# Query and key features of a decoder layer: ten groups from weights stationary to tokens stationary, two at a time, with two of eight pairs of k-tiles by seven products

## The chip, the cores and the metric

The kernel runs on one core of one Trainium2 chip. The metric is the time of one execution on the device, in microseconds (us); the time before is the median of three runs, 1559.32 us (1559.26 to 1560.52). The core has a matrix engine (PE, with PEld loading its stationary operand), a vector engine (DVE), an activation engine (ACT), GpSimd (POOL) and a sync engine (SP) that issues the DMAs here. Matrix products land in PSUM, which the kernel uses as eight banks of 128 x 512 fp32.

## The reference, cut to what matters

One decoder layer, 256 tokens of width 2048, all in fp32:

```
proj = x @ w_in                      # q, k, v, o, gates of the mLSTM; q, k, v of the attention
y_m  = mlstm_mixer(q_m, k_m, v_m, o_m, i_m, f_m, conv, ...)   # conv and silu on q_m, k_m first
y_a  = dilated_attention(q_a, k_a, v_a, rel_bias)
x = layer_norm(ALPHA * x + concat(y_m, y_a) @ w_out)
q, k, v = x @ wq, mem @ wk, mem @ wv     # cross-attention into 256 memory tokens, 4 heads
x = layer_norm(ALPHA * x + softmax(q k^T) v @ wo)
x = layer_norm(ALPHA * x + (silu(x @ w1) * (x @ w3)) @ w2)   # hidden width 5632
```

The change touches six of the eight groups of 512 columns of `w_in` that make queries and keys (groups 2 and 3: attention heads 4 to 7; 4 and 5: query and key of mLSTM heads 0 and 1; 6 and 7: of mLSTM heads 2 and 3), all four groups of `wk`, and the order of one loop over `w2`.

## The kernel before, in words

**Three products for one.** A fp32 product is made of three products in a rounded format. `split` (L109) writes a tile as a high part (ACT) and the rest (DVE subtract); a product is high x high + high x low + low x high. The left operands (tokens) are held split, in an `Operand` (L120): part j holds k-tiles 2j and 2j+1. Weights are loaded as blocks `b` of two k-tiles (1 MB) and split on the fly into `wh` and `wl`, five buffers of each (`SPLIT`, L36), three raw buffers (`RAW`).

**Two layouts.** `gemm_tokens` (L260) keeps tokens stationary and streams 512 columns of weights: the result has tokens on the partitions. `gemm_features` (L382) keeps a 128 x 128 block of weights stationary and streams the tokens: for each k-tile and each of four blocks one matmul of 512 columns (high weights by both parts of the 256 tokens, L392) and one of 256 (low weights by the high tokens, L393). Its result has the features on the partitions, which is what scores, convolution and cross-attention keys want. `features` (L400) adds the two halves. Before, all query and key projections go this way, one group of 512 features at a time.

**Seven products for eight.** `gemm_seven` (L323) makes a 256 x 1024 result as 2 x 2 blocks. For a block `b` in its `plan` that is a plain number it makes the eight block products (24 matmuls of 512 columns); for a block in parentheses, "(b,)", it uses a Winograd-like scheme with seven (21 matmuls): sums of weight blocks are made on DVE (`sums`, L299), sums of token blocks lie ready (`mix`, L136; `mix_again`, L148, makes them from a split operand). It needs all eight PSUM banks: five of the pool `pg` (P2, P3, Q4, E, P1) and all three of the pool `ps` (P5, P7, Q6). After the last seven-step of the plan the function `early` moves P1, P5, P7, Q6 out (`into_rows`, L684, or `into_z`, L665); the other four banks are added at the end. The loop over the feed-forward weights (L988) uses it on two groups at a time, with `plan = [0, 1, (2,), 3, 4, (5,), 6, 7]`, and `hidden` (L946) then makes eight transposes of 128 x 128 on PE (L959). `w2_first` (L976) uses it on the first half of `w2`, twice (w2a0, w2a1).

**Who else wants the three banks of `ps`.** `attention` (L485) takes for each head a bank for the scores (`sc`, L491) and one for their transposes (`pt`, L509), and for each two heads one for the outputs (`po`, L487). `gates` (L523) takes pgate, pc and four times bc. `mlstm` (L598) takes four per head (ms, mh, md, mpt). `turned` (L421) takes one for four transposes.

**What sets the order.** The program is written as one stream; a planner turns it into one fixed order per engine, by its own estimate of when each operand and buffer is ready; among operations that are ready, the earlier in the program goes first. Around the change the stream is: group 0, group 1, values of attention (v0), attention of heads 0 to 3 (L782), groups 2 and 3 (L784), `gates` (L785), attention of heads 4 to 7 (L787), groups 4 and 5 (L801), v1, v2, mLSTM heads 0 and 1 (L818), groups 6 and 7 (L820), mLSTM heads 2 and 3 (L821), keys of the memory 0 and 1 (L834), the output projection (wo0, wo1), keys 2 and 3, the first norm, and so on. Each mLSTM group's convolution (`conv_silu`, L578) runs on DVE as soon as its group is there. SBUF slots of 128 x 1024 are handed out when the program is written, first freed first used.

Of the kernel before, what the change touches and what calls it, by code (L numbers as in the profile page):

```python
# [14 lines left out]
ALU = mybir.AluOpType  # L15
# [7 lines left out]
KT = D // P  # L23
# [27 lines left out]
def decoder_layer(ctx: ExitStack, tc: tile.TileContext, A):  # L51
    nc = tc.nc
    V, SC, G, T = nc.vector, nc.scalar, nc.gpsimd, nc.tensor
# [66 lines left out]
    class Operand:  # L120
# [11 lines left out]
        def put(self, j, src):  # L132

            split(*self.views(j), src.rearrange("p (s t) -> p s t", s=2))
# [65 lines left out]
    def fetch_pair(src, name):  # L200


        def get(b):
            w = wp.tile([P, 2, W], F32, tag="w", name=f"{name}w{b}", bufs=RAW)
            for c in range(2):
                nc.sync.dma_start(
                    out=w[:, :, c * 512 : (c + 1) * 512],
                    in_=src[c][b // 2][:, b % 2].rearrange("p (s c) -> p s c", s=2),
                )
            return w  # L210

        return get
# [169 lines left out]
    def gemm_features(op, src, name, load=None, last=False):  # L382

        banks = [bank(f"{name}b{f}") for f in range(4)]
        for n, wh, wl in weights(src, KT // 2, name, load):
            order = [(f, s) for f in range(4) for s in range(2)]
            if n == 0:
                order.sort(key=lambda x: x[1])
            for f, s in order:
                kt, cs = 2 * n + s, slice(s * 512 + f * P, s * 512 + (f + 1) * P)  # L390
                end = kt == KT - 1
                T.matmul(banks[f], wh[:, cs], op.both(kt), start=kt == 0, stop=end, skip_group_check=True)  # L392
                T.matmul(  # L393
                    banks[f][:, :S], wl[:, cs], op.get(kt, 0), start=False, stop=end, skip_group_check=True
                )
            if last:
                op.free(n)
        return banks

    def features(banks, name):  # L400

        out = []
        for j in range(2):
            t, r = slot(f"{name}t{j}"), slot(f"{name}r{j}")
            for s in range(2):
                cs = slice(s * S, (s + 1) * S)
                SC.copy(t[:, cs], banks[2 * j + s][:, S:])
                V.tensor_tensor(out=r[:, cs], in0=banks[2 * j + s][:, :S], in1=t[:, cs], op=ALU.add)
            free(t)
            out.append(r)  # L410
        return out
# [9 lines left out]
    def turned(rows, j, name):  # L421

        pt = sbank(name)
        for s in range(2):
            for m in range(2):
                at = (2 * j + s) * P
                T.transpose(pt[:, s * S + m * P : s * S + (m + 1) * P], rows[m][:, at : at + P], ident)
        return pt
# [8 lines left out]
        out=tri, in_=tri, pattern=[[1, P]], compare_op=ALU.is_ge, fill=NEG, base=0, channel_multiplier=-1  # L437
# [10 lines left out]
    xT = Operand("xT")  # L448
# [129 lines left out]
    def conv_silu(raw, ft, name):  # L578

        y, t = slot(f"cy{name}"), slot(f"ct{name}")  # L580
        for s in range(2):
            c, a = cw[:, ft + s], s * S
            CONV.tensor_scalar(
                out=y[:, a : a + S], in0=raw[:, a : a + S], scalar1=c[:, 3:4], scalar2=c[:, 4:5],
                op0=ALU.mult, op1=ALU.add,
            )
            for k in range(1, 4):
                CONV.scalar_tensor_tensor(
                    out=y[:, a + k : a + S], in0=raw[:, a : a + S - k], scalar=c[:, 3 - k : 4 - k],
                    in1=y[:, a + k : a + S], op0=ALU.mult, op1=ALU.add,  # L590
                )
# [92 lines left out]
    def into_rows(rows, name):  # L684


        def early(of):
            u = slot(f"{name}u")
            for m in range(2):
                rows.append([slot(f"{name}{m}{c}") for c in range(2)])  # L690
            (r11, r12), (r21, r22) = rows
            SC.copy(r11, of["P1"])
            V.tensor_tensor(out=u, in0=r11, in1=of["Q6"], op=ALU.subtract)
            V.tensor_tensor(out=r21, in0=u, in1=of["P7"], op=ALU.add)
            V.tensor_tensor(out=r12, in0=of["P5"], in1=u, op=ALU.subtract)
            V.tensor_tensor(out=r22, in0=r12, in1=of["P7"], op=ALU.subtract)
            free(u)

        return early

    class Norm:


# [47 lines left out]
        return op  # L751


    def in_features(i, load=None, last=False):
        return features(gemm_features(xT, A["w_qk"][i], f"i{i}", load, last), f"i{i}")

    def in_rows(i):
        return gemm_tokens(xT, A["w_v"][i], KT, f"v{i}")
# [22 lines left out]
    va = rows_of(in_rows(0), "va")  # L781
    for j in range(2):  # L782
        attention(2 * j, qk0[j], qk0[2 + j], [va[m][0] for m in range(2)], tb)
    qk1 = in_features(2) + in_features(3)  # L784
    es, least_norm = gates()  # L785
    free(sel_t)
    for j in range(2):  # L787
# [2 lines left out]

    def mlstm_in(i, h0, last=False):
        q, k = (
            [
                conv_silu(r, at + 2 * (h0 + j), f"{x}{h0 + j}")
                for j, r in enumerate(in_features(i + n, last=last and n == 1))
            ]
            for n, (x, at) in enumerate((("q", 0), ("k", 8)))
        )
        return q, k

# [8 lines left out]
    banks = in_rows(2)  # L809
# [16 lines left out]
    memT, kx = Operand("mT"), Operand("kx")  # L826
    load_mem = loader(memT, A["memT"])

    def keys(g):
        for j, r in enumerate(features(gemm_features(memT, A["xk"][g], f"xk{g}", load_mem), f"xk{g}")):  # L830
            kx.put(2 * g + j, r)
            free(r)

    keys(0)  # L834
    keys(1)


    z = [[slot(f"z{m}{c}") for c in range(4)] for m in range(2)]
# [5 lines left out]
    for g in range(2):  # L844
        banks = gemm_tokens(yT, A["w_out"][g], KT, f"wo{g}", order, last=g == 1)
        for m in range(2):
            ln.add(m, g, banks, stats=False)
    keys(2)
    keys(3)
    for m in range(2):  # L850
        ln.finish(m, stats=True)
    ln.end()
# [119 lines left out]
    banks = gemm_tokens(x2, A["w13_tokens"], KT, "f0", kept=range(HEAD))  # L972
    hidden(0, banks, lambda b, i: [x[:, i * 256 : (i + 1) * 256] for x in b], "f0")
    n, half = FFN // 256, 12

    def w2_first():  # L976
        plan = [0, (2,), 1, (4,), 3, (6,), 5, (8,), 7, 9, 10, 11]
        for c in range(2):
            banks = gemm_seven(
                hT, fetch(A["w2"][c][:half], f"w2a{c}"), 2 * half, f"w2a{c}", plan, into_z(c, ALPHA),  # L980
                last=c == 1,
            )
            for m in range(2):
                add(m, c, banks, scale=1.0)
# [3 lines left out]
    for g in range(2, n, 2):  # L988
        get, rows = fetch_pair(A["w13"][g - 2 : g], f"f{g}"), []
        plan = [0, 1, (2,), 3, 4, (5,), 6, 7]  # L990
        banks = gemm_seven(x2, get, KT, f"f{g}", plan, into_rows(rows, f"f{g}r"), last=g == n - 2)
        for m in range(2):
            for c in range(2):
                V.tensor_tensor(out=rows[m][c], in0=rows[m][c], in1=banks[m][c], op=ALU.add)
        hidden(g, rows, lambda b, i: [b[i][:, x * 256 : (x + 1) * 256] for x in range(2)], f"f{g}")
        free(*rows[0], *rows[1])
        if g == half - 2:
            w2_first()
# [115 lines left out]
```

## Time and profile before

| | |
|---|---|
| median of three runs | 1559.32 us |
| the profiled execution, its own time | 1558.89 us |
| span of the profile (first to last instruction) | 1557.0 us |
| mean granted PE clock | 0.996 |
| busy: PE / DVE / ACT / POOL | 98% / 70% / 48% / 2% |
| matmuls | 7452 |
| DMA moved | 301.33 MB, mean 194 GB/s |

A row of a list in order of time gives the start in us, the duration, the engine, the source line (L392), the operation, the tiles by the program's names (output, then inputs) and shape, with the idle time before it in brackets and what ended that. Matmuls overlap: what one costs a busy PE is the distance from its start to the next one's start, not its duration. A row of the table by stretches gives the bounds, the length, and the busy time and count of PE, PEld, DVE, ACT and POOL, then the granted PE clock, the share of the DMA engines and GB/s.

### The profile page before, as it was taken

The page shows a single profiled execution, that of the slowest core. Times are in us where ns is not written, and L with a number is a line of the kernel's source. Part 1 is how long each engine was busy: PE and PEld are TensorE (multiplying, and loading weights), DVE is VectorE, ACT ScalarE, POOL GpSimd, SP SyncE. Part 2 cuts the span into 40 slices and gives each one's busy share as a digit, 9 for nine tenths or more (in the row PEclk, how much of TensorE's full clock was granted, in tenths as well). Part 3 has the DMA queues.
Part 4 walks back from the last instruction along what each step waited for, and adds up shares of the span by engine and source line. Part 5 has one row for each costly group of instructions (what it writes and reads, how often), then busy time and mean ns, then how long its engine had stood idle before and what let it go on. Part 6 is the DMA issues. An engine that isn't in the chain of part 4 may idle for free.

```text
span 1557.0 us, 19142 instructions
## 1 busy us (share of the span) xinstructions
PE 1533.5 (98%) x7452; PEld 1284.9 (83%) x7452; DVE 1097.5 (70%) x1426; ACT 753.0 (48%) x974; POOL 28.3 (2%) x30
## 2 busy tenths in 40 slices
PE   9999999999999999999998999999899999999997
PEld 7888888888888888888887888887788888888885
DVE  6555774586557655555559678887788778888997
ACT  5445554454433544444434554555446455555551
POOL 0000000000000000000004000000000000000000
PEclk9999999999999999999999999999999999999999
DMA  8664455575554555445553465665465656667552
GB/s 300 238 237 176 150 196 190 185 263 184 200 193 163 201 187 196 180 139 192 188 189 135 163 214 192 216 193 191 147 222 177 205 189 192 214 192 258 199 189 108
DMA packets 83352, 301.33 MB, mean 194 GB/s; under 512 B 7181, under 2 KB 9402, under 8 KB 59710
## 3 DMA queue, kind: packets, MB, share of 16 engines
q1 hardware_dynamic: 83262, 300.12, 56.0%
q8 instruction: 58, 0.95, 0.2%
q14 instruction: 32, 0.26, 0.1%
HBM read 297.97 MB, written 4.21 MB: 194 GB/s over the span
## 4 chain that ended last, share of the span: by engine, by line
PE 96%; DVE 3%; DMA 1%; issue 0%; ACT 0%; SPq 0%; DVEq 0%; ACTq 0%
PE w2a0P L338 2%; PE w2a1P L338 2%; PE w2b0P L338 2%; PE w2b1P L338 2%; PE f10P L338 2%; PE f18P L338 1%; PE f16P L338 1%; PE f14P L338 1%; PE f20P L338 1%; PE f8P L338 1%; PE f12P L338 1%; PE f2P L338 1%; PE f6P L338 1%; PE f4P L338 1%; PE w2a0Q L338 1%; PE w2a1Q L338 1%
## 5 line engine op out<-in xcount | busy, mean ns | idle before, releaser
L257 DVE TENSOR_TENSOR v2l<-v2w,v2h 128x1024 fp32r<-128x1024 f32 x16 | 19.6, 1225 | 21.9 <-ACT v2h L256 21.9
L257 DVE TENSOR_TENSOR v0l<-v0w,v0h 128x1024 fp32r<-128x1024 f32 x16 | 19.6, 1226 | 21.7 <-ACT v0h L256 21.6
L257 DVE TENSOR_TENSOR xv1l<-xv1w,xv1h 128x1024 fp32r<-128x1024 f32 x16 | 19.6, 1225 | 20.7 <-ACT xv1h L256 20.6
L257 DVE TENSOR_TENSOR xv0l<-xv0w,xv0h 128x1024 fp32r<-128x1024 f32 x16 | 19.6, 1226 | 19.9 <-ACT xv0h L256 19.9
L257 DVE TENSOR_TENSOR wo0l<-wo0w,wo0h 128x1024 fp32r<-128x1024 f32 x16 | 19.6, 1226 | 18.7 <-ACT wo0h L256 18.5
L110 ACT CAST w2a1h<-w2a1w 128x1024 fp32r<-128x1024 f32 (+1 forms) x24 | 22.8, 981 | 20.4 <-PE w2a1E L338 11.8
L257 DVE TENSOR_TENSOR xo0l<-xo0w,xo0h 128x1024 fp32r<-128x1024 f32 x16 | 19.6, 1225 | 18.4 <-ACT xo0h L256 18.4
L257 DVE TENSOR_TENSOR wo1l<-wo1w,wo1h 128x1024 fp32r<-128x1024 f32 x16 | 19.4, 1223 | 17.9 <-ACT wo1h L256 17.7
L110 ACT CAST w2a0h<-w2a0w 128x1024 fp32r<-128x1024 f32 (+1 forms) x24 | 22.7, 979 | 16.8 <-PE w2a0E L338 8.2
L256 ACT CAST wo1h<-wo1w 128x1024 fp32r<-128x1024 f32 x16 | 16.8, 1055 | 26.7 <-PE wo1b L276 18.4
L256 ACT CAST f0h<-f0w 128x512 fp32r<-128x512 f32 (+1 forms) x22 | 16.8, 813 | 26.5 <-PE xo1b L276 14.5
L256 ACT CAST v2h<-v2w 128x1024 fp32r<-128x1024 f32 x16 | 16.9, 1055 | 25.2 <-PE v2b L276 18.5
L257 DVE TENSOR_TENSOR v1l<-v1w,v1h 128x1024 fp32r<-128x1024 f32 x16 | 19.6, 1223 | 13.1 <-ACT v1h L256 13.1
L256 ACT CAST v0h<-v0w 128x1024 fp32r<-128x1024 f32 x16 | 16.9, 1054 | 24.6 <-PE v0b L276 19.4
L256 ACT CAST xv1h<-xv1w 128x1024 fp32r<-128x1024 f32 x16 | 16.9, 1055 | 23.8 <-PE xv1b L276 17.2
L111 DVE TENSOR_TENSOR w2a1l<-w2a1w,w2a1h 128x1024 fp32r<-128x1024 f32 (+1 forms) x24 | 26.5, 1130 | 2.5 <-ACT w2a1h L110 2.5
L110 ACT CAST w2b0h<-w2b0w 128x1024 fp32r<-128x1024 f32 (+1 forms) x20 | 19.2, 988 | 17.0 <-PE w2b0E L338 10.1
L256 ACT CAST xv0h<-xv0w 128x1024 fp32r<-128x1024 f32 x16 | 16.9, 1054 | 21.6 <-PE xv0b L276 16.4
L256 ACT CAST wo0h<-wo0w 128x1024 fp32r<-128x1024 f32 x16 | 16.9, 1054 | 21.3 <-PE wo0b L276 15.0
L111 DVE TENSOR_TENSOR w2a0l<-w2a0w,w2a0h 128x1024 fp32r<-128x1024 f32 (+1 forms) x24 | 26.4, 1129 | 0.9 <-ACT w2a0h L110 0.9
L338 PE MATMUL w2a0P<-w2a0h,hT 128*128 128x512 f32 x80 | 26.8, 395 | 0.0
L256 ACT CAST xo0h<-xo0w 128x1024 fp32r<-128x1024 f32 x16 | 16.8, 1051 | 20.4 <-PE xo0b L276 16.2
(1388 smaller groups left out, 5431.6 us busy)
## 6 DMA issues: line engine op xcount, KB each, us to landing
w2a0w<-in_w SPq DMA_DIRECT2D x12, 1024.0 KB, 5.0
w2a1w<-in_w SPq DMA_DIRECT2D x12, 1024.0 KB, 4.9
w2b0w<-in_w SPq DMA_DIRECT2D x10, 1024.0 KB, 5.0
w2b1w<-in_w SPq DMA_DIRECT2D x10, 1024.0 KB, 4.9
v0w<-in_w_v SPq DMA_DIRECT2D x8, 1024.0 KB, 5.1
v1w<-in_w_v SPq DMA_DIRECT2D x8, 1024.0 KB, 4.9
v2w<-in_w_v SPq DMA_DIRECT2D x8, 1024.0 KB, 4.9
wo0w<-in_w_out SPq DMA_DIRECT2D x8, 1024.0 KB, 4.9
```

The costliest lines, as they stand in the source:

```text
L110: SC.copy(hi, src)
L111: V.tensor_tensor(out=lo, in0=src, in1=as_f32(hi), op=ALU.subtract)
L256: SC.copy(wh[:, cs], w[:, i, cs])
L257: eng.tensor_tensor(out=wl[:, cs], in0=w[:, i, cs], in1=as_f32(wh[:, cs]), op=ALU.subtract)
L338: T.matmul(of[to], lhsT, rhs, start=to not in begun, stop=end)
```

## The change

Groups 2 and 3, 4 and 5, 6 and 7 of the input projection and keys 0 and 1, 2 and 3 are each made together by `gemm_seven`, tokens stationary, with the plan `[0, 1, 2, (3,), 4, (5,), 6, 7]`. The sums of token blocks for parts 3 and 5 are made once for `xT` and once for `memT`. Afterwards the 256 x 1024 result is put together in SBUF (`whole`) and turned back to features by sixteen transposes (`turned`, four times), each bank then copied by ACT or split into the keys. The convolution of a query group now comes after its key group too. The loads of `memT` are all written ahead of the first weights of the keys. In `w2_first` the plan is changed so that the first seven-step comes after three plain blocks, and two plain blocks instead of four follow the last.

```diff
+    def whole(rows, banks):
+        for m in range(2):
+            for c in range(2):
+                V.tensor_tensor(out=rows[m][c], in0=rows[m][c], in1=banks[m][c], op=ALU.add)
+
+    def by_feature(op, src, name, put, load=None, last=False):
+
+        get, rows, plan = fetch_pair(src, name), [], [0, 1, 2, (3,), 4, (5,), 6, 7]
+        if load:
+            for i in range(KT // 2):
+                load(i)
+        for i in (3, 5):
+            if i not in op.mixed:
+                op.mix_again(i)
+        banks = gemm_seven(op, get, KT, name, plan, into_rows(rows, f"{name}r"), last=last)
+        whole(rows, banks)
+        for c in range(2):
+            for i in range(2):
+                put(c, i, turned([rows[m][c] for m in range(2)], i, f"{name}p{c}{i}"))
+            free(*(rows[m][c] for m in range(2)))
+
...
+    def two_in_features(i, last=False):
+        out = [[None] * 2 for _ in range(2)]
+
+        def put(c, j, pt):
+            out[c][j] = slot(f"i{i + c}{j}")
+            SC.copy(out[c][j], pt)
+
+        by_feature(xT, A["w_qk"][i : i + 2], f"i{i}", put, last=last)
+        return out
...
-    qk1 = in_features(2) + in_features(3)
+    qk1 = sum(two_in_features(2), [])
...
-            for n, (x, at) in enumerate((("q", 0), ("k", 8)))
+            [conv_silu(r, at + 2 * (h0 + j), f"{x}{h0 + j}") for j, r in enumerate(raw)]
+            for (x, at), raw in zip((("q", 0), ("k", 8)), two_in_features(i, last))
...
-    keys(0)
-    keys(1)
+    by_feature(memT, A["xk"][0:2], "xk0", lambda c, i, pt: kx.put(2 * c + i, pt), load_mem)
...
-    keys(2)
-    keys(3)
+    by_feature(memT, A["xk"][2:4], "xk2", lambda c, i, pt: kx.put(4 + 2 * c + i, pt))
+    free(*memT.mixed.values())
+    memT.mixed.clear()
...
     def w2_first():
-        plan = [0, (2,), 1, (4,), 3, (6,), 5, (8,), 7, 9, 10, 11]
+        plan = [0, 1, 3, (2,), 5, (4,), 7, (6,), 9, (8,), 10, 11]
```

More of the change, by code (lines that the diff above doesn't have):

```diff
@@ L751, in transposed, with in_features @@
         return op
-    def in_features(i, load=None, last=False):
-        return features(gemm_features(xT, A["w_qk"][i], f"i{i}", load, last), f"i{i}")
+    def in_features(i, load=None):
+        return features(gemm_features(xT, A["w_qk"][i], f"i{i}", load), f"i{i}")
+    def two_in_features(i, last=False):
[5 more added lines that the diff above has]
+        return out
     def in_rows(i):
@@ L792, in mlstm_in @@
         q, k = (
[L793 to L796, printed above, removed]
-            for n, (x, at) in enumerate((("q", 0), ("k", 8)))
+            [conv_silu(r, at + 2 * (h0 + j), f"{x}{h0 + j}") for j, r in enumerate(raw)]
+            for (x, at), raw in zip((("q", 0), ("k", 8)), two_in_features(i, last))
         )
@@ L827, in decoder_layer @@
     load_mem = loader(memT, A["memT"])
[L829 to L832, printed above, removed]
-    keys(0)
-    keys(1)
+    by_feature(memT, A["xk"][0:2], "xk0", lambda c, i, pt: kx.put(2 * c + i, pt), load_mem)
     z = [[slot(f"z{m}{c}") for c in range(4)] for m in range(2)]
@@ L991, in decoder_layer @@
         banks = gemm_seven(x2, get, KT, f"f{g}", plan, into_rows(rows, f"f{g}r"), last=g == n - 2)
-        for m in range(2):
-            for c in range(2):
-                V.tensor_tensor(out=rows[m][c], in0=rows[m][c], in1=banks[m][c], op=ALU.add)
+        whole(rows, banks)
         hidden(g, rows, lambda b, i: [b[i][:, x * 256 : (x + 1) * 256] for x in range(2)], f"f{g}")
```

## The prediction

> **What bounds the kernel now.** I read the page's table of engines and the chain that ended last first. (0.2%, 3.1 us, is about what a measurement of this kernel can tell from no change.)
>
> ```profile
> span 1557.0 us, 19142 instructions
> PE 1533.5 (98%) x7452; PEld 1284.9 (83%) x7452; DVE 1097.5 (70%) x1426; ACT 753.0 (48%) x974; POOL 28.3 (2%) x30
> PE 96%; DVE 3%; DMA 1%; issue 0%; ACT 0%; SPq 0%; DVEq 0%; ACTq 0%
> ```
>
> PE is the chain. So an edit counts by the PE time that it adds or removes, and by the waits that it puts before PE. The stretches show the cover that PE's partners have: first the stages that change (attention groups 2-3; gates and groups 4-5; groups 6-7; keys 0-1), then v2, a feed-forward pair in full and one without `hidden`, then w2a0 and w2a1.
>
> ```profile
> 97.40:148.60 51.20, 51.20 (x301) 45.04 (x300) 32.62 (x54) 26.17 (x47) 0.00 (x0) 1.00 0.51 181
> 148.60:204.10 55.50, 55.50 (x328) 47.58 (x327) 40.01 (x78) 32.07 (x59) 0.00 (x0) 1.00 0.44 152
> 295.30:346.10 50.80, 50.80 (x303) 44.94 (x302) 38.83 (x72) 25.95 (x40) 1.41 (x2) 1.00 0.66 229
> 346.10:398.20 52.10, 52.10 (x314) 46.16 (x313) 36.64 (x72) 24.44 (x37) 1.38 (x2) 1.00 0.58 206
> 250.40:295.30 44.90, 44.90 (x205) 37.34 (x204) 21.53 (x20) 19.01 (x21) 0.00 (x0) 1.00 0.54 188
> 1226.00:1268.00 42.00, 42.00 (x187) 34.80 (x186) 29.87 (x32) 20.33 (x21) 0.00 (x0) 1.00 0.62 200
> 1092.81:1163.38 70.57, 66.38 (x285) 53.48 (x284) 57.04 (x66) 33.59 (x38) 0.00 (x0) 0.95 0.51 179
> 1163.38:1225.90 62.52, 62.52 (x277) 51.79 (x276) 52.33 (x57) 31.99 (x33) 0.00 (x0) 1.00 0.58 202
> ```
>
> PE is busy for the whole of every stage that changes, with DVE at 64 to 76%. Only w2a0 stands out.
>
> **The change, part 1: matmuls and transposes.** In order of time, two stretches of group 2 (first and last of 14 and of 8 large matmuls, each followed by its small one), then the starts of two feed-forward pairs in the chain.
>
> ```profile
> 113.28 0.39 PE L392 MATMUL i2b<-xT,i2h 128*128 128x512 f32 x1
> ...
> 117.78 0.39 PE L392 MATMUL i2b<-xT,i2h 128*128 128x512 f32 x1
> ...
> 119.82 0.40 PE L392 MATMUL i2b<-xT,i2h 128*128 128x512 f32 x1
> ...
> 122.30 0.40 PE L392 MATMUL i2b<-xT,i2h 128*128 128x512 f32 x1
> ```
>
> ```profile
> 919.37 5.44 PE f4P L338 x24
> ...
> 962.48 5.44 PE f6P L338 x24
> ```
>
> One large and one small matmul cost 4.50/13 = 0.346 us in the first stretch, 2.48/7 = 0.354 in the second. A group has 64 such pairs, so two groups cost 44.3 to 45.3 us; I take 44.8. By sevens they cost 6 x 24 + 2 x 21 = 186 matmuls of 5.44/24 = 0.2267, which is 42.16. A feed-forward pair is the same 186 matmuls and eight transposes: 962.48 - 919.37 = 43.11, so a transpose with its share of the break in the stream costs 0.95/8 = 0.119. Sixteen cost 1.9. Two groups: 44.8 - 42.16 - 1.9 = 0.74 gained (0.2 to 1.2), five times: **-3.7 us** (-1 to -6). DMAs move the same bytes, in halves of the blocks as the feed-forward pairs do, at the same share; nothing there.
>
> **Part 2: w2_first.** w2a0 takes 70.57 us, w2a1 62.52 for the same matmuls (276 x 0.2267 = 62.6). Eight transposes of `hidden` take 0.95 of the 8.05, and 7.1 is waiting, partly at half clock. The waits:
>
> ```profile
> PE w2a0P L338 <- ACT w2a0h L110: 2.5, 1, 2.5
> PE w2a0P L338 <- DVE w2a0l L111: 1.1, 1, 1.1
> ```
>
> Its first seven-step follows after one plain block (24 x 0.2267 = 5.4 us) while DVE and ACT still do `hidden`. With three plain blocks ahead there are 16.3 us, more than the two blocks that every feed-forward pair has there, in which the table shows PE without a gap (42.00 of 42.00). I take the 7.1 as gone. The other end of the plan loses cover: after the last seven-step come two plain blocks, 10.9 us, for `early`, two blocks' splits and the sums into z. The feed-forward pairs do this with two, with DVE at 71% (29.87 of 42.00); w2 has 84% (52.33 of 62.52). I take 1 us (0 to 2). Sum **-6.1 us** (-7.1 to -5).
>
> **Part 3: the three banks of `ps`.** This decides. How are these banks handed out? Rows of attention in order of time (scores, transposes, outputs of head 0, scores of head 1; transposes of head 3; then gates, the last of its bc, the scores of head 4, the transposes of head 7), and from DVE's list the last input of head 4's scores.
>
> ```profile
> 97.38 0.59 PE L492 MATMUL sc<-i0r,i0t 128*128 128x256 f32 x2
> ...
> 105.03 0.27 PE L510 MATMUL pt<-ident,va 128*128 128x128 f32 x1
> ...
> 109.41 0.59 PE L516 MATMUL po<-va,sel 128*128 128x256 f32 x2
> ...
> 110.06 0.60 PE L492 MATMUL sc<-i0r,i0t 128*128 128x256 f32 x2
> ...
> 139.72 0.27 PE L510 MATMUL pt<-ident,apT 128*128 128x128 f32 x1
> ...
> 148.68 0.28 PE L527 MATMUL pgate<-xT,gw 128*40 128x256 f32 x1
> ...
> 167.92 1.12 PE L564 MATMUL bc<-g,tb 4*128 4x256 f32 x4
> ...
> 171.63 0.59 PE L492 MATMUL sc<-va,i2t 128*128 128x256 f32 x2
> ...
> 226.15 0.27 PE L510 MATMUL pt<-ident,i2r 128*128 128x128 f32 x1
> ```
>
> ```profile
> 150.99 0.42 DVE L408 TENSOR_TENSOR i3r<-i3b,i2t 128x256 f32<-128x256 f32 x1
> ```
>
> Head 1's scores need only the features of groups 0 and 1, there long before 97.38, and head 0 held one bank of three. Yet they start at 110.06, straight after head 0's outputs. Head 4's inputs are ready at 151.4, and its scores wait until 171.63, straight after the last bc. Attention stands earlier in the program than the matmuls that PE does meanwhile, so readiness was not lacking: a bank is promised in the order in which the program first uses it. In that order P5, P7 and Q6 of groups 4-5 come after the transposes of head 7, and those of groups 2-3 after the transposes of head 3.
>
> How long can PE do without P5? Ahead of it lie blocks 0, 1, 2 (72 matmuls), block 4 (24), and of each seven-step P1, P2, P3 and Q4 (12): 120 x 0.2267 = 27.2 us, plus whatever attention or gates ask. Behind that, four of the five split buffers are held by the steps that wait (two each); the last 48 matmuls have one. A k-tile then costs, in sequence, ACT's copy, DVE's subtract and twelve matmuls:
>
> ```profile
> 102.33 1.05 ACT L256 CAST i2h<-i2w 128x1024 fp32r<-128x1024 f32 x1 [0.40 <-PE i2b L392]
> ```
>
> ```profile
> 103.42 1.23 DVE L257 TENSOR_TENSOR i2l<-i2w,i2h 128x1024 fp32r<-128x1024 f32 x1 [0.52 <-ACT i2h L256]
> ```
>
> That is 1.05 + 1.23 + 2.72 = 5.0 us instead of 2.7; four of them lose 9.1 us at most. At the end 18 matmuls remain, and `early` and `whole` come last instead of beside block 6 and 7.
>
> Groups 2-3: head 3's transposes came 42.3 us after the scores of head 0. PE has 27.2 us and about 6 of attention's own, so it starves from 33 on, for 9 us at half speed, then some cover at the end is gone: 3 us (1 to 5). Groups 4-5: gates to head 7's transposes took 226.15 - 148.68 = 77.5 us, spread over groups 4, 5 and v1; now it must fit beside groups 4-5. PE has 27.2 and about 9 of gates and attention, 36 us. What is left of the chain then is about 40 us at the old pace; with ACT and DVE half idle I take it at 25 (a head's chain is scores to outputs, 12.0 us above, in which PE's fixed order waited for nothing). In those 25 us PE gets 11 of gemm and 5 of attention done: 9 lost, less the 3 of attention's PE work that v1 no longer has, 6 (3 to 14). Groups 6-7 and keys 0-1:
>
> ```profile
> 325.81 0.60 PE L642 MATMUL mpt<-ident,mw 128*128 128x128 f32 x4
> ...
> 363.84 1.50 PE L603 MATMUL ms<-i6r,i7r 128*128 128x128 f32 x12
> ...
> 397.12 0.38 PE L642 MATMUL mpt<-ident,k 128*128 128x128 f32 x2
> ```
>
> mLSTM head 1's last bank is asked for 30.5 us into groups 6-7, just when PE runs out: 1 us (0 to 3). In keys 0-1 head 3's last came 51 us in, of which 17.7 before its first scores were convolution of the keys alone. Now the queries' convolution falls there too, and DVE, which had 36.64 of 52.10 us, gets this (head for head the same operations), the two token sums and about 9 more (29.87 in a pair, 21.53 in v2 with as many plain splits as two groups): over 50. I take 5 us (1 to 8). Keys 2-3 have no bank user ahead. Sum **+15 us** (5 to 30).
>
> All: -3.7 - 6.1 + 15 = +5.2 on the profiled execution's 1558.89 us (its span 1557.0 and 1.9 around it), which lies 0.4 below the median: **1564.5 us**. The bounds give 1558.9 - 6 - 7.1 + 5 = 1550.8 and 1558.9 - 1 - 5 + 30 = 1582.9.
>
> [...] Rows of PE in w2a0, the only stage with gaps:
>
> ```profile
> 1104.68 1.22 PE L338 MATMUL w2a0P<-w2a0h,hTm 128*128 128x512 f32 x2 [2.46 <-ACT w2a0h L110]
> ...
> 1108.03 0.63 PE L338 MATMUL w2a0P<-w2a0l,hTm 128*128 128x512 f32 x1
> ...
> 1108.46 0.63 PE L338 MATMUL w2a0P<-w2a0h,hTm 128*128 128x512 f32 x1
> ```
>
> After a gap of 2.46 us matmuls are 0.43 apart instead of 0.227, and the stage's clock was 0.95. The starving stretches above have gaps of about 2.3 us. [...]
>
> **The rivals.** (a) The banks come in time: freed of the convolution of group 4 and of the planner's slack, attention runs in half of its old time, PE never starves, and of part 3 at most 6 us are left. For it: head 0's outputs started at 109.41, although its transposes were through at 105.3. Time 1558.9 - 9.8 + (0 to 6) = 1549 to 1555, faster. It decides where a head needs under 6 us. (b) Gain and waits cancel: waits of 6.5 to 12.7 us give 1555.8 to 1562; the same. (c) The forecast's waits but with the clock falling in the starving stretches of groups 4-5 and keys 0-1: four k-tiles in each at 5.4 instead of 2.7, +22, so 1586; slower. (d) The plan of w2 does not do what it should, since `hidden`'s slots hold it up and not the plan: +6 on any of these; inside the forecast's range.
>
> **How the numbers follow.** Forecast (waits of 13 us and more, clock full) 0.48, rival a 0.26, b 0.18, c 0.08. Faster 0.26, same 0.18, slower 0.56. The range 1551 to 1582 leaves out c and the tails; the forecast's own range is 1562 to 1582.
>
> **What would show it.** Right: in groups 4-5 P5's first matmul straight after head 7's transposes, a stage of 60 us or more with PE waiting for ACT or DVE of single k-tiles; keys 0-1 near 57; w2a0 at about 63.5. Wrong: sevens of groups 4-5 begun before attention is through, so that banks are not promised in order; or stages of 51 us with PE full, which makes part 3 nothing; or w2a0 still at 70.

## The result, and the profile after

The change takes 1598.96 us (median of four runs, 1595.97 to 1601.2) against 1559.92 for the kernel before on the same chip: ratio 1.0249, 95% interval 1.0226 to 1.0272. It is slower, as forecast, but by 39 us where 5 were forecast, outside the range. The runs of the change lie at two values, 1596 and 1601; the last section comes back to this. The profiled run took 1595.97 us. Its page, the totals and the chain that ended last:

```profile
span 1594.2 us, 18726 instructions
...
PE 1544.9 (97%) x7182; PEld 1274.8 (80%) x7182; DVE 1154.8 (72%) x1496; ACT 763.5 (48%) x971; POOL 29.1 (2%) x30
...
PE 90%; DVE 7%; DMA 1%; issue 1%; ACT 1%; SPq 0%; DVEq 0%; POOL 0%; ACTq 0%
```

There are 270 matmuls fewer, PE is nevertheless busy for longer, and of the chain DVE now has 7%. To see where, I cut both profiles at the same first matmuls. Stretch A runs from the first scores of head 0 (groups 2-3 start there) to v2; stretch K from groups 6-7 through keys 0-1, wo0 and wo1 to keys 2-3; then all up to w2a0; then w2a0. The kernel before, then the change, to which keys 0-1 by itself is added:

```profile
97.30:250.50 153.20, 153.20 (x838) 131.17 (x837) 103.59 (x176) 80.34 (x135) 0.00 (x0) 1.00 0.50 176
295.30:485.30 190.00, 190.00 (x999) 163.25 (x998) 122.58 (x190) 86.32 (x112) 2.79 (x4) 1.00 0.59 206
...
485.30:1092.70 607.40, 602.18 (x2971) 506.95 (x2971) 414.96 (x522) 291.88 (x384) 22.11 (x16) 1.00 0.54 184
1092.70:1163.20 70.50, 66.31 (x286) 53.39 (x285) 56.97 (x66) 33.59 (x38) 0.00 (x0) 0.95 0.51 179
```

```profile
97.80:267.00 169.20, 156.95 (x730) 124.85 (x729) 124.10 (x200) 85.55 (x135) 0.00 (x0) 1.00 0.46 155
311.80:524.90 213.10, 196.49 (x891) 162.38 (x890) 147.44 (x221) 91.50 (x109) 3.70 (x4) 0.96 0.56 188
...
360.40:436.00 75.60, 58.99 (x260) 48.06 (x259) 59.79 (x112) 29.90 (x40) 2.29 (x2) 0.89 0.52 175
...
524.90:1135.30 610.40, 604.58 (x2917) 505.15 (x2916) 425.30 (x531) 292.02 (x380) 22.09 (x16) 1.00 0.54 183
1135.30:1200.60 65.30, 64.45 (x285) 52.32 (x284) 53.97 (x63) 33.43 (x38) 0.00 (x0) 1.00 0.55 193
```

| stretch | before | after | measured | forecast, parts 1 to 3 |
|---|---|---|---|---|
| A: groups 2-3, gates, groups 4-5, v1 | 153.2 | 169.2 | +16.0 | 3 + 6 - 1.5 = +7.5 |
| v2 | 44.8 | 44.8 | 0 | 0 |
| K: groups 6-7, keys 0-1, wo0, wo1 | 190.0 | 213.1 | +23.1 | 1 + 5 - 1.5 = +4.5 |
| keys 2-3 up to w2a0 | 607.4 | 610.4 | +3.0 | -0.7 |
| w2a0 | 70.5 | 65.3 | -5.2 | -6.1 |

These sum to +36.9 of the 37.2 between the spans. The two stretches have 29 us of standing still between them (169.20 - 156.95 and 213.10 - 196.49), and keys 0-1, 75.6 us long, had the clock at 0.89, which is worth at most 0.11 x 75.6 = 8 us more (less, where the slow time falls into the stops).

Groups 4-5, PE in order of time: their first matmul, the scores of head 4, the first stop, and the last transposes (`pt`) with the first of twelve products on token sums behind them:

```profile
151.93 0.39 PE L338 MATMUL i4P<-i4h,xT 128*128 128x512 f32 x1
...
187.51 0.59 PE L492 MATMUL sc<-va,i2r 128*128 128x256 f32 x2
...
189.00 0.50 PE L338 MATMUL i4Q<-i4h,xT 128*128 128x512 f32 x1 [0.67 <-ACT i4h L110]
...
212.50 0.27 PE L512 MATMUL pt<-ident,i 128*128 128x128 f32 x1
212.53 0.48 PE L338 MATMUL i4P<-i4h,xTm 128*128 128x512 f32 x1
...
217.97 0.50 PE L338 MATMUL i4Q<-i4h,xTm 128*128 128x512 f32 x1 [1.06 <-DVE yT L111]
```

This is the picture that the prediction drew: single k-tiles awaited from ACT (the next such stop has 1.34 us), P5 at 212.53 straight after head 7's transposes, and Q6 waiting for DVE to read head 7's outputs (`yT`), which lie in the bank that it is to get. Keys 0-1 in the same view:

```profile
379.77 0.39 PE L338 MATMUL xk0P<-xk0h,mT 128*128 128x512 f32 x1
387.48 2.90 PE L603 MATMUL ms<-cyq,q 128*128 128x128 f32 x12 [7.32 <-DVE q L594]
...
397.17 0.44 PE L642 MATMUL mpt<-ident,k 128*128 128x128 f32 x2 [1.93 <-ACT k L640]
397.44 2.70 PE L603 MATMUL ms<-q,q 128*128 128x128 f32 x12
...
408.41 0.79 PE L338 MATMUL xk0Q<-xk0h,mT 128*128 128x512 f32 x1 [5.44 <-ACT xk0h L110]
...
412.50 0.63 PE L642 MATMUL mpt<-ident,q 128*128 128x128 f32 x2
412.79 0.78 PE L338 MATMUL xk0P<-xk0h,mTm 128*128 128x512 f32 x1
```

The same order of banks (412.79 behind head 3's `mpt`), but longer stops: 7.32 us for the last convolution ahead of head 2 (`ms`) and 5.44 for a split of weights. Between 380 and 408 PE did little but the heads' own products: it was busy for 11.95 of the 28.00 us.

### The profile page after: what moved, and what is told of

It is laid out like the page before. It is cut to its first block, busy times and chain, and to the rows that moved or that the text cites. A ratio compares the mean times of both kernels' runs of the same rounds, so it can differ in the third digit from the quotient of the medians.

```text
span 1594.2 us, 18726 instructions
## 1 busy us (share of the span) xinstructions
PE 1544.9 (97%) x7182; PEld 1274.8 (80%) x7182; DVE 1154.8 (72%) x1496; ACT 763.5 (48%) x971; POOL 29.1 (2%) x30
## 4 chain that ended last, share of the span: by engine, by line
PE 90%; DVE 7%; DMA 1%; issue 1%; ACT 1%; SPq 0%; DVEq 0%; POOL 0%; ACTq 0%
PE w2a1P L338 2%; PE w2a0P L338 2%; PE w2b0P L338 2%; PE w2b1P L338 2%; PE f10P L338 1%; PE i6P L338 1%; PE f18P L338 1%; PE f16P L338 1%; PE f20P L338 1%; PE f14P L338 1%; PE f8P L338 1%; PE f6P L338 1%; PE f4P L338 1%; PE f2P L338 1%; PE f12P L338 1%; PE i4P L338 1%
## 5 line engine op out<-in xcount | busy, mean ns | idle before, releaser
L257 DVE TENSOR_TENSOR wo1l<-wo1w,wo1h 128x1024 fp32r<-128x1024 f32 x16 | 19.4, 1222 | 17.9 <-ACT wo1h L256 17.7
L257 DVE TENSOR_TENSOR xo1l<-xo1w,xo1h 128x512 fp32r<-128x512 f32 (+1 forms) x22 | 19.5, 929 | 11.9 <-ACT xo1h L256 11.8
L256 ACT CAST xo1h<-xo1w 128x512 fp32r<-128x512 f32 (+1 forms) x22 | 17.0, 816 | 20.9 <-PE xo1b L276 8.4
L110 ACT CAST i6h<-i6w 128x1024 fp32r<-128x1024 f32 (+1 forms) x16 | 15.8, 1000 | 22.8 <-PE i6E L338 16.1
L111 DVE TENSOR_TENSOR i6l<-i6w,i6h 128x1024 fp32r<-128x1024 f32 (+1 forms) x16 | 18.2, 1156 | 11.6 <-ACT i6h L110 11.6
```

The lines of the kernel that those rows point to most:

```text
L110: SC.copy(hi, src)
L111: V.tensor_tensor(out=lo, in0=src, in1=as_f32(hi), op=ALU.subtract)
L256: SC.copy(wh[:, cs], w[:, i, cs])
L257: eng.tensor_tensor(out=wl[:, cs], in0=w[:, i, cs], in1=as_f32(wh[:, cs]), op=ALU.subtract)
```

## The experiments

Four theories were in play at the end. Theory 1: the products P5, P7 and Q6 wait for the banks of `ps`, promised in program order to earlier heads. The rivals: features come late, since a pair delivers only at its end; DVE and ACT have too much to do; and, formed on the way, theory 4: the new sums wait for SBUF slots, which are promised in program order as well. Each ratio is against runs of the kernel before on the same chip. The expectations say VectorE for DVE, ScalarE for ACT and local memory for SBUF.

**The plan of `w2_first` alone**, on the kernel before:

```diff
-        plan = [0, (2,), 1, (4,), 3, (6,), 5, (8,), 7, 9, 10, 11]
+        plan = [0, 1, 3, (2,), 5, (4,), 7, (6,), 9, (8,), 10, 11]
```

> The kernel before with the new plan of w2_first and nothing else. The prediction's step: -6.1 us, so 1553.8. The profile after shows w2a0 to w2a1 at 65.3 us instead of 70.6, so 1554.6 if the gain belongs to the plan; the rival (hidden's slots hold w2a0 up, not the plan) has no change, 1559.9.

1553.63 us (1553.22 to 1553.93), ratio 0.9962, interval 0.9947 to 0.9977. In its profile w2a0 has 65.40 us instead of 70.50, at full clock:

```profile
1093.00:1158.40 65.40, 64.53 (x286) 52.40 (x286) 54.17 (x63) 33.45 (x38) 0.00 (x0) 1.00 0.54 193
```

It is faster than both kernels, and the fastest of the versions here. So the feature pairs cost 45 us, not 39.

**Attention written after the pairs**: heads 0 to 3 behind groups 2-3, heads 4 to 7 behind groups 4-5.

```diff
+    qk1 = sum(two_in_features(2), [])
     for j in range(2):
         attention(2 * j, qk0[j], qk0[2 + j], [va[m][0] for m in range(2)], tb)
-    qk1 = sum(two_in_features(2), [])
...
     q0, k0 = mlstm_in(4, 0)
+    for j in range(2):
+        attention(4 + 2 * j, qk1[j], qk1[2 + j], [va[m][1] for m in range(2)], tb)
```

> The changed kernel, with attention of heads 0 to 3 written after groups 2 and 3, and that of heads 4 to 7 after groups 4 and 5; same work. Theory of the banks (P5, P7, Q6 wait for every earlier user of the three banks): these users now come later, so the stretch from the end of v0 to the start of v2 falls from 168.7 us to about the 152.5 of before: about 1583. Rival (late features: two groups at a time deliver their features only at the end of the pair, and all that hangs on them is late; or the added work of DVE): attention is not earlier than it was and DVE has the same work, so no gain, 1597 to 1601.

1605.12 us (1600.68 to 1610.54), ratio 1.0299, interval 1.027 to 1.0328: a miss. Groups 2-3, the one pair of it with no bank user ahead, then the stage behind it:

```profile
97.00:139.40 42.40, 42.40 (x189) 35.11 (x188) 31.74 (x35) 20.74 (x22) 0.00 (x0) 1.00 0.64 218
139.40:207.70 68.30, 60.24 (x292) 48.03 (x291) 40.33 (x70) 34.96 (x64) 0.00 (x0) 0.98 0.33 108
```

The pair itself takes 42.40 us, PE without a gap. But its neighbours' banks are only moved: groups 4-5 now have heads 0 to 3 and the gates ahead of them in the program, and PE stands still there for 8 us. The 6 us more than the change lie in K (219.9 us at a clock of 0.91), which this edit does not touch.

**mLSTM heads 2 and 3 written after keys 0-1** instead of before:

```diff
-    for h in range(2):
-        mlstm(2 + h, q1[h], k1[h], vm, gate, es[2 + h], least_norm)
-    free(*vm[0], *vm[1], *gate[0], *gate[1])
...
     by_feature(memT, A["xk"][0:2], "xk0", lambda c, i, pt: kx.put(2 * c + i, pt), load_mem)
+    for h in range(2):
+        mlstm(2 + h, q1[h], k1[h], vm, gate, es[2 + h], least_norm)
+    free(*vm[0], *vm[1], *gate[0], *gate[1])
```

> The changed kernel, with mLSTM heads 2 and 3 written after keys 0 and 1; same work. Theory of the banks: keys 0 and 1 fall from 75.6 us to 48 to 55, less what the output projection now waits for its last eight k-tiles (0 to 10): 1575 to 1585. Rival (DVE is saturated by four convolutions, two token sums and the weights' sums at once): the same work of DVE in the same stretch, keys 0 and 1 stay above 65: above 1588.

1597.93 us (1597.56 to 1603.19), ratio 1.0254, interval 1.0238 to 1.027: again nothing gained. Stretch K, the time ahead of keys 0-1, and keys 0-1:

```profile
316.50:529.30 212.80, 191.90 (x892) 159.48 (x891) 148.33 (x221) 92.52 (x110) 2.79 (x4) 0.95 0.55 188
...
365.00:388.80 23.80, 2.92 (x19) 1.89 (x17) 21.54 (x45) 6.85 (x11) 0.00 (x0) 0.65 0.33 104
388.80:433.00 44.20, 44.18 (x187) 36.38 (x188) 34.16 (x45) 23.34 (x27) 0.00 (x0) 0.95 0.60 201
```

With the banks free keys 0-1 runs in 44.20 us, PE full. But it starts 23.80 us late. What for? The rows of PE and of ACT's splits of the memory's tokens (`mT`):

```profile
388.82 0.79 PE L338 MATMUL xk0P<-xk0h,mT 128*128 128x512 f32 x1 [19.77 <-ACT mT L110]
```

```profile
L110 ACT CAST mT<-q x3: 617/618/619, 388.2 to 392.7; 128x512 fp32r<-128x512 f32 x3
...
L110 ACT CAST mT<-i4r x2: 617/618/618, 387.2 to 391.4; 128x512 fp32r<-128x512 f32 x2
```

The profile prints a slot by a name it has borne: the raw tokens lie in slots of `q` and `i4r`, tensors of the convolutions. By this reading their loads waited until DVE, busy for 21.54 of those 23.80 us, had done those. Slots are handed out by the program "first freed first used", so what asks late in the program gets the slots that were freed last. That is theory 4.

**The pairs by eight plain blocks**: two groups together, tokens stationary, turned, with the new plan of `w2_first`, but no sevens, no sums and no banks of `ps` for the products.

```diff
-        banks = gemm_seven(op, get, KT, name, plan, into_rows(rows, f"{name}r"), last=last)
-        whole(rows, banks)
+        banks = [[bank(f"{name}b{m}{c}") for c in range(2)] for m in range(2)]
+        for b in range(KT // 2):
+            for n, wh, wl in plain(get, b, name):
...
+        rows = rows_of(banks, f"{name}r")
```

> The changed kernel, with all eight blocks of each pair by eight products: no bank of the small pool is taken by the matmuls, no sums of weights or tokens; two at a time, tokens stationary and turned as in the change. Theory of the banks: the waits go, six matmuls of 0.227 come per pair: 1559.9 - 5.3 + 5 x (192 x 0.2267 + 1.9 - 44.7) = about 1558. Rival (late features): the convolution of four tiles still comes in one piece behind the pair, keys 0 and 1 stay near 70 us: 1580 or more.

1559.21 us (1558.83 to 1559.56), ratio 0.9996, interval 0.9987 to 1.0006. Stretches A and K:

```profile
97.30:252.60 155.30, 155.30 (x741) 127.87 (x741) 94.05 (x150) 78.90 (x127) 0.00 (x0) 1.00 0.50 170
299.50:489.10 189.60, 189.60 (x889) 158.40 (x888) 119.13 (x169) 86.41 (x102) 2.99 (x3) 1.00 0.62 210
```

The features come as late here as in the change, and PE has no gap. Late features fall as a cause by themselves; the loss belongs to the sevens.

**The same, with the work of the sevens done and not used**: token sums, weight sums and their splits, six sums at the end, none of it read by a matmul.

```diff
+        for i in (3, 5):
+            if i not in op.mixed:
+                op.mix_again(i)
...
+            if b in (3, 5):
+                unused(get, b, name)
```

> The pairs by eight plain blocks of the run before this (1559.2 us), to which VectorE and ScalarE are given back what the sevens ask of them: token sums of two blocks, the sums of two weight blocks and their splits into buffers that no matmul reads, and six sums at the end. PE does exactly what it did there, and no product waits for a bank of `ps`. This work is done and not used. Theory 1 (the three products wait for the banks that earlier attention and mLSTM heads hold in program order): the added work fits beside PE, 1559 to 1567 us. Rival (VectorE and ScalarE are too full once the sums fall on the same stages as the convolutions): most of the 39 us come back, 1580 to 1600 us.

1591.1 us (1588.71 to 1592.0), ratio 1.0197, interval 1.0182 to 1.0212. No product of it is in `ps`, and most of the loss is back: the rival's number. But only in one place:

```profile
96.70:251.90 155.20, 155.20 (x743) 128.12 (x742) 119.21 (x184) 85.88 (x134) 0.00 (x0) 1.00 0.60 199
298.70:513.70 215.00, 197.54 (x889) 164.04 (x889) 149.65 (x213) 94.98 (x112) 3.15 (x3) 0.94 0.60 204
```

A keeps its 155 us with DVE busy for 119 instead of 94: there the sums are hidden, and what the change lost in A is not their work. K has 215 instead of 190. The rows that end PE's stop in keys 0-1, and DVE's first weight sum:

```profile
364.57 0.61 PE L744 MATMUL xk0b<-xk0h,mT 128*128 128x512 f32 x2
372.58 2.93 PE L603 MATMUL ms<-cyq 128*128 128x128 f32 x12 [7.39 <-DVE cyq L594]
...
395.90 2.08 PE L740 MATMUL xk0b<-xk0h,mT 128*128 128x512 f32 x4 [5.83 <-ACT xk0h L110]
```

```profile
389.34 1.23 DVE L710 TENSOR_TENSOR xk0t<-xk0w 128x1024 f32<-128x1024 f32 x1 [0.23 <-PE mh L616]
```

The plain block that PE wants after 364.57 is split behind the first sum, and that sum waits for `mh`, an mLSTM product that is no input of it. By the program's list its slot held the mLSTM's values, which `mh` reads: the slot is what it waits for. That this is the cause is put to the test below.

**The loads first**: heads 2 and 3 after keys 0-1, and the memory's loads written ahead of the convolutions.

```diff
+    raw = two_in_features(6, True)
+    memT, kx = Operand("mT"), Operand("kx")
+    load_mem = loader(memT, A["memT"])
+    for i in range(KT // 2):
+        load_mem(i)
+    q1, k1 = (
+        [conv_silu(r, at + 2 * (2 + j), f"{x}{2 + j}") for j, r in enumerate(rr)]
+        for (x, at), rr in zip((("q", 0), ("k", 8)), raw)
+    )
```

> As the run with mLSTM heads 2 and 3 written after keys 0-1 (1597.9 us), but the loads of the memory's tokens are written ahead of the convolutions of those heads, so that they take other slots of the local memory than the ones that the convolutions free. In that run PE stood still for 23 us ahead of keys 0-1, waiting for the first split of those tokens, and then did keys 0-1 in 44 us without a gap. Theory 1: the hole goes, keys 0-1 stays at 44 to 46 us, so 1597.9 - 23 + 0 to 4 for the heads that now fall beside the output projection: 1574 to 1580 us. Rival (VectorE too full for convolutions and sums together, whatever the banks): the hole turns into gaps inside keys 0-1, 1590 us or more.

1588.65 us (1588.51 to 1591.95), ratio 1.019, interval 1.0173 to 1.0207. The right way, 9 us of the 18 to 24 expected: stretch K is 203.2 us, and of the hole 4.5 us for `mT` and 2.1 for its sums are left among the waits.

**The sevens late**: plan `[0, 1, 2, 4, 6, (3,), (5,), 7]` in the pairs.

> The change with the plan of the pairs at five plain blocks, then the two seven-steps, then one plain block, instead of three, a seven, one, a seven, two. PE has 38 us of work ahead of the first product in `ps` instead of 27. Theory 1: up to 10.9 us less of what is lost in groups 4-5 and in keys 0-1, less 1 to 3 us in each pair for the cover that is gone at its end: 1577 to 1590 us. Rival (VectorE's and ScalarE's work is what delays PE, the banks are free by then): the same work in the same stages, 1597 to 1605 us.

1585.42 us (1585.0 to 1585.93), ratio 1.0163, interval 1.0148 to 1.0178. Stretch K has 203.90, 9.2 less; A has 171.00, no less. It puts off everything that the sevens wait for, banks and slots alike, so it does not tell them apart. For A it is a miss of theory 1: P5 of groups 4-5 still starts straight behind head 7's transposes (213.70), and PE stands still for 12 us as before (171.00 - 159.03), now more at the heads' own transposes, which wait for DVE (4.1 us for `i` and 2.0 for `apT`, where the change has 2.3 for `i` and 1.0 for `va`). Why the added cover does not help there stays open.

**Convolution by head**: queries and keys of head 2, head 2, then those of head 3.

```diff
+    for h in range(2):
+        q, k = (conv_silu(r[h], at + 2 * (2 + h), f"{x}{2 + h}") for (x, at), r in zip((("q", 0), ("k", 8)), raw))
+        mlstm(2 + h, q, k, vm, gate, es[2 + h], least_norm)
```

> The change with one edit: of heads 2 and 3 of the mLSTM, the queries and keys of head 2 are convolved, head 2 is written, and then those of head 3, instead of all four convolutions first. Theory 1 with late features as its second half (the banks are held by heads whose inputs come late, in one piece of 19 us on VectorE): head 2 starts 9 us earlier, and keys 0-1 gets shorter by 5 to 10 us, 1588 to 1594 us. Rival 2 (the lateness of the features does not matter, or VectorE's total does): 1597 to 1600 us.

1597.24 us (1595.51 to 1599.51), ratio 1.024, interval 1.0224 to 1.0255. The wait of `ms` fell from 7.3 to 2.4 us, and stretch K stayed at 212.90: the longest wait on the page was not the one that decided.

**Unused work, slots of its own**: the run with unused sums, with the memory's tokens, their sums and the weights' sums taken first from the list, so that they get slots that were idle before heads 2 and 3.

```diff
+    def memory_in(op, src):
+        spare = [big(f"xk0x{i}", F32) for i in range(2)]
+        mixes = {i: big(f"{op.name}m{i}") for i in (3, 5)}
+        stage, work = (big(f"{op.name}w{i}", F32) for i in range(2))
+        for j in range(KT // 2):
+            raw = stage[:, j % 2 * 512 : (j % 2 + 1) * 512]
+            nc.sync.dma_start(out=raw, in_=src[j])
+            op.put(j, raw)
+            if j in mixes:
+                op.mix_again(j, (mixes[j], work))
+        free(stage, work)
+        return spare
```

> The run with the sums computed and not used (1591.1 us, keys 0-1 78 us instead of 49, no product in `ps`), with one edit in keys 0-1: the memory's tokens, their sums and the sums of the weights get slots of the local memory that were free before mLSTM heads 2 and 3, taken in another order from the same list. In that run they got slots that held the inputs and scratch of those heads. The work of every engine is the same. Theory 4 (a slot, like a bank, is promised in program order; the first sums wait for the heads' inputs to be dropped, and the blocks behind them on ScalarE and VectorE wait too): keys 0-1 goes back to 49 to 54 us, 1562 to 1568 us. Rival (it is the amount of VectorE and ScalarE work): 1583 us or more.

1574.26 us (1572.53 to 1575.47), ratio 1.0089, interval 1.0074 to 1.0104: 17 of the 32 us are gone with no work taken away, between the two expectations. Stretch K:

```profile
299.60:499.40 199.80, 193.64 (x889) 160.53 (x888) 148.71 (x212) 95.06 (x112) 2.08 (x3) 0.97 0.67 221
```

So 15.2 of the 25.4 us that K had more were slots; 10.2 are left there, for the work itself and its order.

**The change, slots of its own**: the same edit on the change; the banks stay as they are.

> The change, with the same reordering of slots in keys 0-1 and nothing else; its products still wait for the banks of heads 2 and 3. If slots alone held keys 0-1 up: 75.6 us become 46 to 52 and the time 1570 to 1576 us. If banks hold it up by themselves as well (theories 1 and 4 both): P5 still cannot start before head 3's transposes, some 45 us into the stage or later; 62 to 72 us for the stage, 1584 to 1595 us. If neither matters: 1598 us.

1602.46 us (1598.6 to 1604.08), ratio 1.0267, interval 1.0252 to 1.0282: no gain, and more even than "neither matters" said. The 3.5 us above the change lie in A, which this edit does not touch (177.0 us in this profile, 169.2 in the change's). K, then head 2's scores and P5, again straight behind head 3's `mpt`:

```profile
319.00:532.60 213.60, 200.00 (x891) 161.07 (x891) 147.39 (x221) 91.26 (x109) 2.79 (x4) 0.96 0.55 187
```

```profile
411.25 2.76 PE L609 MATMUL ms<-cyq,q 128*128 128x128 f32 x12
...
433.24 0.44 PE L648 MATMUL mpt<-ident,q 128*128 128x128 f32 x2
433.43 0.48 PE L344 MATMUL xk0P<-xk0h,mTm 128*128 128x512 f32 x1
```

DVE is now busy without a gap from the start of keys 0-1 (367.57) to head 2's scores, with token sums and splits between the steps of the convolutions. So these scores come 43.7 us into the stage instead of 27.1, head 3's `mpt` and P5 come later with them, and nothing is gained.

**Both taken away**: slots of its own, and heads 2 and 3 after keys 0-1. The loads, splits and sums of the tokens are also written ahead of the convolutions, as the loads were in the run with the loads first.

> The change with both taken away in keys 0-1: mLSTM heads 2 and 3 written after it, so that no bank is promised ahead of its products, and its tokens and sums in slots that were free before. As the run with the loads first (1588.7 us), whose remaining hole of 8 us ahead of keys 0-1 and waits for the token sums inside were slots still. Theories 1 and 4: no hole, the stage at 44 to 46 us, 1574 to 1582 us. Rival (VectorE's work): 1588 us or more.

1583.92 us (1580.01 to 1586.46), ratio 1.0144, interval 1.0127 to 1.016. A and K:

```profile
97.40:275.00 177.60, 162.68 (x729) 129.06 (x729) 124.20 (x200) 85.22 (x135) 0.00 (x0) 0.96 0.45 149
319.80:515.30 195.50, 192.57 (x892) 158.29 (x891) 147.03 (x221) 90.88 (x110) 2.79 (x4) 0.99 0.61 205
```

The hole is gone, as expected, but the time is 2 us above the range. In the profiled run, the longest of the four (1586.46 us), the reason stands in A, which this edit does not touch: 177.60 us in the first row, 169.20 in the change's profile (last section). By K the four cases are:

| stretch K, us (190.0 before) | banks behind heads 2, 3 | banks free |
|---|---|---|
| sums and tokens in late slots | 213.1 (the change) | 212.8 |
| in slots of their own | 213.6 | 195.5 |

In these profiles either wait alone costs all of it; without both, 17.6 of the 23.1 us are gone. That is why taking away one at a time showed nothing. DVE's work by itself is not the reason: in the last run DVE is as full (44.8 of the 44.8 us of keys 0-1, 369.5 to 414.3), and PE, which has no head's bank to wait for, is busy for 42.2 of them. (With the banks free and only the tokens' loads early, the run with the loads first, K is 203.2.)

**Pairs only from group 6 on**: as the last one, with groups 2 to 5 by single groups of features.

```diff
-    qk1 = sum(two_in_features(2), [])
+    qk1 = in_features(2) + in_features(3)
```

> As the run before with slots and banks taken out of keys 0-1's way (1583.9 us), but groups 2-3 and 4-5 by single groups of features as in the kernel before, so that no pair is left whose products queue behind another stage's banks. By the stages measured: the stretch from groups 2-3 to v2 goes from 177 us back to 153, the rest stays: 1584.7 - 24.5 = 1560 us of span, 1558 to 1565 us in all, still above the plan of w2_first alone (1553.6 us), since groups 6-7 to the output projection took 195.5 us there against 190.0 before and keys 2-3 with what follows 2.9 us more. If the banks are not what groups 2 to 5 lose by, their loss was something that follows the pairs elsewhere, and the time stays above 1570 us.

1559.73 us (1558.61 to 1560.46), ratio 0.9998, interval 0.9989 to 1.0008. As expected:

```profile
97.70:250.90 153.20, 153.20 (x838) 131.16 (x837) 103.45 (x179) 79.78 (x133) 0.00 (x0) 1.00 0.49 172
295.70:487.70 192.00, 190.51 (x891) 157.47 (x891) 148.44 (x227) 90.59 (x110) 3.70 (x4) 1.00 0.62 206
```

A is what it was, K is 2.0 us above the kernel before, and keys 2-3 with what follows up to w2a0 take 611.7 us against 607.4, most of what the plan of `w2_first` gains. So even with both waits out of the way these pairs gain nothing here.

## Why the prediction was right in direction and wrong in size

**Part 2** was right in its sum: -6.1 forecast, -6.0 measured alone (1553.63 against 1559.62); the rival that the plan would not help falls. Part of the agreement is luck. By the profiles w2a0 gained 5.1 us (70.50 to 65.40) where 7.1 was forecast, and w2a1 lost 0.1 (62.52 to 62.60) where 1 was.

**Part 1** was right for what PE does: 42.16 us of matmuls for a pair, 42.40 measured where no bank was held (attention after the pairs). What it called a gain, 3.7 us for five pairs, is nearer to 1: by eight plain blocks the five pairs cost 5.6 us over the plan alone (1559.21 - 1553.63), and the 30 matmuls that sevens save are worth 30 x 0.2267 = 6.8 (an estimate from these runs). The change shows none of it: with the waits gone, K is still at 192.0 to 195.5 against 190.0.

**Part 3, A.** The mechanism was right: banks are promised in program order. PE was to run out 36 us into groups 4-5 and to have 25 us of the chain still ahead. It first stood still after 36.4 us (189.00 - 0.67 - 151.93), and the last of head 7's transposes came 24.2 us later, at 212.50. The size was off by a factor of two, 7.5 forecast and 16.0 measured. Of these 12.3 us are PE standing still. The stretch around that chain, in the change:

```profile
184.00:214.00 30.00, 24.02 (x113) 18.48 (x111) 17.61 (x36) 16.76 (x41) 0.00 (x0) 1.00 0.32 110
```

It has 6 us of stops (30.00 - 24.02), where 9 were forecast. But from the 9 the forecast took off 3 for attention's PE work that v1 no longer has. That work was already among the 16 us that it let PE do in the 25, so the 3 were taken off twice. Of the other stops 3.2 us stand in groups 2-3, where 3 were forecast, and 3.0 behind 214, in the end of the pair and v1, where nothing was. The remaining 3.7 us are PE time, where 1.5 less was forecast. The pairs without sevens have 2.1 us more in A than before, too, but they have twelve matmuls, 2.7 us, more than the change; what the change's PE time comes from is not shown. That the stops are the banks, and not DVE's sums, follows from the run with unused sums, which keeps 155.20, and from the 42.40.

**Part 3, keys 0-1: the step that failed.** "I take 5 us (1 to 8)" became 23.5 (52.1 to 75.6). Three things were missing. First, the slots: the sums and the memory's tokens were costed as work for DVE, and not as tiles that need a place. Second, the waits were taken as a share of a chain that goes on meanwhile. But PE's order is fixed: it stood at head 2's scores for 7.32 us and could not take up the k-tiles behind them. These scores came 27.1 us into the stage instead of 17.7, behind the queries' convolution, which the forecast named but did not price as a wait. By the table of four cases these two are priced only together: 17.6 of K's 23.1 us go when both waits are taken away, and none when one is. Third, the clock: 0.89 over the stage, at most 8 us. That was rival (c), given 0.08, with 22 us for two stages. It came true in one of them in this profile, beside the forecast's waits and not instead of them.

**Keys 2-3**, without a bank user ahead, were taken as gaining 0.7; with what follows they lost 3.0.

**Rivals (a) and (b)**, banks in time or cancelling, fall: the banks were in time only in groups 6-7, where PE is busy for all of 48.60 us (311.80 to 360.40) and 1 us of waiting was forecast. The range failed since its upper end, 30 us for part 3, came from the same list of waits as the forecast: a resource left out of the sum was left out of the bounds, too.

**The clock.** In keys 0-1 the granted clock was 0.54 from 387.4 to 391.0 us, after the stop of 7.32 us, and 0.50 from 408.4 to 412.8, after the one of 5.44; both stops are longer than the 2.3 that the forecast reckoned with. But it was also 0.55 from 397.2 to 400.3, after a stop of 1.93: the twelve matmuls of head 3's scores at 397.44 take 2.70 us, and the twelve at 363.84 in the profile before took 1.50. The forecast's sum took its waits at full clock. That stops of about 2.3 us leave it full is shown by no run; what the profiles show is both outcomes after shorter stops: 0.55 after the 1.93 us above and 1.00 (545 to 571) after 1.93 us ahead of 549.21 in keys 2-3, and both again after 1.34 us in the last section.

**Left open:** how the 2 to 10 us that stay in K with banks and slots free divide between DVE's work and its order. Nothing here separates them.

## What to carry to other kernels

A form that does fewer matmuls can need resources that the old one did not: here three more banks, and slots for sums, mixed tokens and rows, both handed out in program order, so that the new products queue behind whoever stands earlier in the text. Count every buffer that a new step asks for, find its last user in the program, and ask when that one is through; work that "fits beside" an engine has to find its place first. And where two waits lie over each other, undoing one can show nothing, as here: try both together before a theory is dropped.

## What the runs showed of the hardware that was not expected

The same program up to v2 took 169.20 us for stretch A in one profile and 177.60 in another. The change, then the run with both taken away, PE after the same stop for the same split (the line numbers are shifted by six):

```profile
190.84 0.74 PE L338 MATMUL i4P<-i4h,xT 128*128 128x512 f32 x2 [1.34 <-ACT i4h L110]
...
191.88 0.62 PE L338 MATMUL i4Q<-i4h,xT 128*128 128x512 f32 x2
192.33 0.61 PE L338 MATMUL i4P<-i4l,xT 128*128 128x512 f32 x2
192.79 0.62 PE L338 MATMUL i4P<-i4h,xT 128*128 128x512 f32 x2
```

```profile
196.11 0.73 PE L344 MATMUL i4P<-i4h,xT 128*128 128x512 f32 x2 [1.34 <-ACT i4h L110]
...
197.15 0.96 PE L344 MATMUL i4Q<-i4h,xT 128*128 128x512 f32 x2
197.90 1.05 PE L344 MATMUL i4P<-i4l,xT 128*128 128x512 f32 x2
198.76 1.05 PE L344 MATMUL i4P<-i4h,xT 128*128 128x512 f32 x2
```

After the same stop of 1.34 us pairs of matmuls stay 0.46 us apart in one run, and get 0.86 apart in the other, a microsecond after PE is busy again. So with the same program a stretch with many short stops fell to about half its pace in one profile (0.86 us from pair to pair against 0.46) and kept it in the other, and the length of the last stop does not tell which. The clock of the second run was 0.96 over all of A; PE was busy there for 5.7 of the 8.4 us more (162.68 against 156.95) and stood still for the rest. Four more profiles with the same program up to v2 lie between the two, in the order of their clocks: 171.8 (convolution by head) and 172.4 us (loads first) at 0.99, 174.2 (mLSTM after keys 0-1) at 0.98, 177.0 (slots of its own) at 0.96. The change's two longer runs fit this, with a clock of 0.985 and 0.989 over the whole run against 0.992 and 0.991, but only a shorter one was profiled. What decides stays open.
